# Seven merge-gate tiles of each layer move from the attention's filling into the rotary stage

## The chip, the cores and the metric

The kernel runs on one core of a Trainium2 chip. A core has five engines with an instruction queue each: TensorE (PE: matrix products; PEld is its weight load), VectorE (DVE), ScalarE (ACT), GpSimd (POOL) and SyncE (SP), which here only issues transfers. The metric is the device time of one execution in microseconds, lower is better.

## The reference

Two layers of a mixer act on 1024 tokens of a prompt and on 32 tokens of a running stream (1056 columns in all), with 1024 channels in float32. The part that matters here:

```
h = rmsnorm(x) * (1 + scale) + shift
u_a, z_a, b_a, a_a, q_b, k_b, v_b, z_b, g_a, g_b = split(h @ w_in)
o_a = gated_delta_rule(conv_silu(u_a), ...)      # branch A: a triangular inverse per chunk, a scan over chunks
q_b, k_b = rope(q_b), rope(k_b)                  # branch B: differential attention, 8 heads of two maps
o_b = softmax1(q_b k_b) v - lam * softmax2(...) v
merged = sigmoid(g_a) * (o_a @ w_proj_a) + sigmoid(g_b) * (o_b @ w_proj_b)
x = x + gate * (merged @ w_out)
```

Each of g_a and g_b has 1024 columns, that is eight tiles of 128. The change is about seven of the eight tiles of g_a.

## The kernel before, in words

Activations lie channel by channel, in three groups of tokens (384, 384 and 288 columns), each split into a high and a low part; a product in full precision is three products (high x high, high x low, low x high). One tile of a projection (128 output columns, 1024 channels, one token group) is thus 8 x 3 = 24 products into one PSUM bank. Weights come as float32 (`wraw`) and are split into `whi` (ScalarE) and `wlo` (GpSimd or VectorE).

A layer runs through these stages:

- A: for each of eight heads the projections of u_a, the convolution, and `k.T @ [k q]` in three passes (`ptk`, L599 on), which VectorE and ScalarE write to `rec` (two buffers, stored at L622) and `U` (stored as `ublk`, L629). Rotary pair 0 is already emitted here.
- B, the rotary stage: `rope_pair` (L786) for pairs 1 to 7, four of queries and keys each by turns (odd pairs are keys). For a token group it has two tiles `pr` of 24 products (L813 on); VectorE multiplies each by cosine and sine (`rt`, four a group); GpSimd makes two `ro` of the four; they are stored, and for keys TensorE transposes them (`ptk`, L830). Beside it `invert` (L646) inverts 128 unit lower triangles of 64 x 64, one to a partition: 63 steps, each an `itmp` (product) and an `X` (subtraction), the first 26 columns on VectorE, the others on GpSimd, and a copy `ub<-X` (L668) at its end. Two sections of eight steps are emitted after each pair; the instruction order on every engine is settled by a scheduler when the program is built.
- C1: merging the inverses, and the scan over chunks. Its first product is that of the values, `ptok`, which stands behind everything in B.
- C2: the attention, whose products wait for softmax on ScalarE and VectorE. TensorE's order is written out by hand in C1 and C2: `pad` takes independent products from a list of fillers (values, the gate tiles z_b, g_a, g_b, z_a by `zproj`, L1154, in the bank `pd`, and branch A's projection) and puts them between the attention's steps. What is left (`s.left`) is spread in equal shares over what is still to come, and `s.pad(1e9)` runs the remainder at the end.
- E, F: attention's projection, the merge, the output projection, and the next layer's norm.

PSUM has eight banks. Two of them belong to the pool `pd` (projections of all kinds, `pr` and `ptok` among them) for the whole program; the other pools are opened and closed by stage. A stage's pool that takes the banks of an earlier one waits for the last reader there. Small results (`ro`, `rt`, `zo`) share the eight buffers of the pool `ev`.

Of the kernel before, what the change touches and what calls it, by code (L numbers as in the profile page):

```python
# [10 lines left out]
F32 = mybir.dt.float32  # L11
F32R = mybir.dt.float32r
# [6 lines left out]
L = 2  # L19
# [19 lines left out]
class Net:  # L39
# [39 lines left out]
    def setup(s, st):  # L79
# [3 lines left out]
        s.pd = P("pd", 2, space=PSUM)  # L83
# [34 lines left out]
    def conditions(s, tmp):  # L118
        """The two conditioning vectors, channel by channel."""
# [86 lines left out]
    def pad(s, ns):  # L206
        """Independent products, as far as there are any, for this long on the tensor engine."""
# [20 lines left out]
    def mod_init(s, pool):  # L228
        """The two conditioning vectors, both parts of each, as stationary columns."""
# [9 lines left out]
    def mod_chunk(s, l, part, c):  # L239
        """256 columns of shift (part 0), scale (1) or gate (2), by channel."""  # L240
# [19 lines left out]
    def mod_gate(s, l):  # L260
        """The gate's rows, halved for the gates' 1 + tanh."""
# [9 lines left out]
    def mod_first(s, part, c, pool, wpool):  # L271
        """256 columns of the first layer's shift or scale, in plain float32."""
# [24 lines left out]
    def start(s, h, pool, wpool, xpool):  # L297
        """The first layer's activations, channel by channel as its scale and shift arrive."""
# [50 lines left out]
    def rstd(s, pool, ss, n, scale, add):  # L349
        """(ss * scale + add) ** -0.5; add: a number or an AP."""  # L350
# [17 lines left out]
    def norm_tile(s, pool, l, x, t, h, r):  # L368
# [12 lines left out]
        h = h if isinstance(h, list) else h(g)  # L381
# [8 lines left out]
    def gates(s, l, pool, h):  # L390
# [28 lines left out]
        # beta = 1 / (1 + exp(-b))  # L419
# [6 lines left out]
        # g = -exp(a_log) * softplus(a + dt_bias)  # L426
# [83 lines left out]
    def conv_head(s, l, pool, h, hd, cv, gates=None):  # L510
        """q, k and v of one head; with `gates`, the last token group comes after the others."""
# [33 lines left out]
    def gdn1(s, l, pool, h, hd, cv, gates=None):  # L545
# [5 lines left out]
        # token-major k, v and the squares of q and k  # L551
# [19 lines left out]
        # 1/|k| and its uses  # L571
# [13 lines left out]
        # q with its decay, channel-major  # L585
# [60 lines left out]
    def invert(s, l, pool):  # L646
        nc = s.nc
        for B, nb, src, xd, pdst in ((64, 128, s.ublk[l], s.xblk[l], s.pblk[l]), (32, H, s.ublks[l], None, s.pblks[l])):
# [25 lines left out]
    def merge_inverse(s, l, pool, hd):  # L674
        """The off-diagonal quarter of each chunk's inverse, and all of it to the scan's records."""
# [24 lines left out]
    def scan(s, l, pool, gap):  # L700
        """One (chunk, head) after the other; each one's three stages start a turn apart."""
# [9 lines left out]
        def first(c, hd):  # L711
# [11 lines left out]
            if c == 0:  # L723
                # the prompt's state is zero before it
# [61 lines left out]
    def rope_pair(s, l, pool, wpools, h, c_base, pr, dst, tabs, out):  # L786
        """Four (head, map) groups: tile A has their first halves, tile B the second ones."""
        nc = s.nc
        W = []
        for kk in range(2):  # L790
# [6 lines left out]
            if not out:  # L797
                # the queries' factor, a power of two
# [10 lines left out]
        for g, (t0, n) in enumerate(GROUPS):  # L809
# [3 lines left out]
            for e in range(2):  # L813
# [3 lines left out]
                for x, tab in enumerate((cos, sin)):  # L817
                    tmp = s.ev.tile([128, 384], F32, tag="ev", name=f"rt{e}{x}")
                    s.tt(tmp[:, :n], ps[:, :n], tab[:, sl], OP.mult)
                    tm.append(tmp)  # L820
            s.tt(o[0][:, :n], tm[0][:, :n], tm[3][:, :n], OP.subtract, eng=nc.gpsimd)
# [719 lines left out]
```

## Time and profile before

| | |
|---|---|
| runs | 3727.11, 3731.49, 3732.44 us (median 3731.49) |
| span of the profiled execution | 3730.3 us |
| busy share of the span | TensorE 93%, VectorE 62%, ScalarE 41%, GpSimd 37% |
| mean granted TensorE clock | 0.973 of full speed |
| stage B of layer 0, first `ptk` of the last head to first `ptok` | 526.7 to 750.3 us |
| the same of layer 1 | 2338.8 to 2561.2 us |
| attention C2, layers 0 and 1 | 1096 to 1731 us, 2870 to 3539 us |

The profiled execution is one of its own; its span is the time that the sums are made against, and the median of the runs is what a change is measured by. TensorE's share is a mean over stages: it is nearly full in C1, C2, E and F, and less so in A and B.

### The profile page before, as it was taken

The numbers are of one execution on the slowest core, as the hardware profiler recorded it, in microseconds if no ns is written. First come the engines' busy times: TensorE is split into PE (matmuls) and PEld (weight loads), VectorE is DVE, ScalarE is ACT, GpSimd is POOL, SyncE is SP. The second block draws the span as 40 slices with busy tenths as digits, with TensorE's granted clock in tenths as the row PEclk, the third lists the DMA queues.
The fourth block names the chain that finished last, engine by engine and source line by source line (L and its number), as shares of the span: only waits on it lengthen the run. The fifth ranks groups of instructions, "written<-read, shape, count | busy, mean of one in ns | idle before, by whom it ended". The sixth has DMA issues, their size and how long they took to land.

```text
span 3730.3 us, 58279 instructions
## 1 busy us (share of the span) xinstructions
PE 3465.2 (93%) x20752; PEld 3122.7 (84%) x20752; DVE 2301.0 (62%) x3874; ACT 1525.3 (41%) x4246; POOL 1370.8 (37%) x1259
## 2 busy tenths in 40 slices
PE   8888897899999999899999998879999999989999
PEld 6888897878978888789988888878898888878897
DVE  5677758832436667865456676787043666777554
ACT  4566541123534444433244656211354444444421
POOL 2456548701143343423002223792111443343310
PEclk9999999999999999999999999989999999999999
DMA  5445544266743334445443434424775333444554
GB/s 176 118 143 149 144 122 120 78 185 202 229 114 89 118 114 128 143 136 177 139 144 92 120 114 118 134 79 135 204 225 158 101 110 107 131 139 142 171 155 149
DMA packets 611307, 518.01 MB, mean 139 GB/s; under 512 B 103444, under 2 KB 563864, under 8 KB 610632
## 3 DMA queue, kind: packets, MB, share of 16 engines
q1 hardware_dynamic: 611016, 514.29, 46.7%
q8 instruction: 164, 2.69, 0.3%
q14 instruction: 127, 1.04, 0.1%
HBM read 333.84 MB, written 180.31 MB: 138 GB/s over the span
## 4 chain that ended last, share of the span: by engine, by line
PE 50%; DMA 9%; DVE 9%; POOL 4%; issue 4%; ACT 2%; SPq 1%; DVEq 0%; POOLq 0%; ACTq 0%
PE pd L72 25%; PE ptok L72 9%; PE psc L72 5%; PE pts L72 2%; PE pav L72 2%; DMA Gb<-grow 2%; DMA srec<-grec 2%; PE po L72 1%; PE pr L72 1%; PE pta L76 1%; DMA kraw<-kscr 1%; DVE qh L942 1%; DMA er<-rrow 1%; PE ptm L72 1%; POOL X L54 1%
## 5 line engine op out<-in xcount | busy, mean ns | idle before, releaser
L72 PE MATMUL pd<-h,whi 128*128 128x384 f32 (+1 forms) x5376 | 1405.8, 337 | 35.1 <-ACT u L69 28.5
L72 PEld LDWEIGHTS pd<-h,whi 128*128 128x128 f32 x5376 | 947.4, 193 | 61.5 <-ACT u L69 30.7
L72 PE MATMUL pd<-h,wlo 128*128 128x384 f32 (+1 forms) x2688 | 902.6, 336 | 0.0
L54 POOL TENSOR_TENSOR wlo<-wraw,whi 128x512 fp32r<-128x512 f32 (+1 forms) x220 | 432.6, 1975 | 503.9 <-ACT whi L69 461.1
L72 PEld LDWEIGHTS pd<-h,wlo 128*128 128x128 f32 x2688 | 516.9, 192 | 11.8 <-issue 8.1
L72 PE MATMUL pr<-h,whi 128*128 128x384 f32 (+1 forms) x1536 | 389.1, 338 | 30.5 <-DVE rt L54 30.4
L69 ACT CAST whi<-wraw 128x1024 fp32r<-128x1024 f32 (+1 forms) x304 | 259.3, 866 | 227.8 <-PE pd L72 77.8
L66 ACT ACTIVATE e<-psc,nm 32x160 f32<-32x160 f32 (+8 forms) x288 | 200.7, 700 | 290.0 <-DVE nm L1016 168.3
L72 PEld LDWEIGHTS pr<-h,whi 128*128 128x128 f32 x1536 | 279.0, 197 | 39.2 <-DVE rt L54 37.9
L72 PE MATMUL pr<-h,wlo 128*128 128x384 f32 (+1 forms) x768 | 257.8, 336 | 0.7 <-POOL wlo L54 0.7
L63 DVE SCALAR_TENSOR_TENSOR acc<-u,convT,acc 128x1059 f32<-128x1059 f32 x144 | 220.7, 1536 | 2.7
L72 PE MATMUL pd<-oa,whi 128*128 128x384 f32 (+1 forms) x768 | 196.2, 334 | 3.9 <-DVE egt L63 3.9
L72 PE MATMUL pd<-ob,whi 128*128 128x384 f32 (+1 forms) x768 | 181.9, 322 | 4.6 <-DVE egt L63 4.6
L54 DVE TENSOR_TENSOR wlo<-wraw,whi 128x1024 fp32r<-128x1024 f32 x84 | 107.6, 1281 | 121.3 <-ACT whi L69 121.2
L72 PE MATMUL ptok<-whi,h 128*128 128x512 f32 x512 | 164.8, 401 | 5.7 <-DVE rt L54 5.7
L54 DVE TENSOR_TENSOR itmp<-ub,X 128x624 f32<-128x624 f32 (+56 forms) x188 | 152.5, 811 | 15.3 <-DMA ub<-ublks 6.5
L72 PE MATMUL ptok<-whi,mg 128*128 128x512 f32 x512 | 158.7, 392 | 1.0 <-DVE y L54 1.0
L54 DVE TENSOR_TENSOR X<-X,itmp 128x624 f32<-128x624 f32 (+56 forms) x188 | 153.6, 817 | 5.0
L54 POOL TENSOR_TENSOR ro<-rt,rt 128x384 f32<-128x384 f32 (+1 forms) x96 | 115.5, 1222 | 102.5 <-issue 53.9
L72 PE MATMUL psc<-k,qh 128*128 128x512 f32 (+3 forms) x416 | 150.6, 394 | 2.3 <-ACT e L66 2.1
L72 PE MATMUL psc<-k,ql 64*128 64x512 f32 (+3 forms) x416 | 152.4, 448 | 0.0
L72 PEld LDWEIGHTS pr<-h,wlo 128*128 128x128 f32 x768 | 151.3, 197 | 1.1 <-POOL wlo L54 1.1
(308 smaller groups left out, 7121.8 us busy)
## 6 DMA issues: line engine op xcount, KB each, us to landing
wraw<-in_w_in SPq DMA_DIRECT2D x160, 512.0 KB
srec<-grec SPq DMA_DIRECT2D x128, 384.0 KB
grec<-rec SPq DMA_DIRECT2D x128, 192.0 KB
z<-zo SPq DMA_DIRECT2D x96, 192.0 KB
wraw<-in_w_ada SPq DMA_DIRECT2D x64, 256.0 KB
egt<-z SPq DMA_DIRECT2D x64, 192.0 KB
eo<-ob SPq DMA_DIRECT2D x60, 192.0 KB
Gb<-grow SPq DMA_DIRECT2D x16, 576.0 KB
```

The source lines that it names most:

```text
L54: (eng or s.nc.vector).tensor_tensor(out, a, b, op=op)
L63: s.nc.vector.scalar_tensor_tensor(out, a, sc, b, op0=op0, op1=op1)
L66: s.nc.scalar.activation(out, a, func, **kw)
L69: s.nc.scalar.copy(out, a)
L72: s.nc.tensor.matmul(out, lhsT, rhs, start=start, stop=stop)
L76: s.nc.tensor.transpose(out, a, s.ident[0:n, 0:n])
L942: s.nc.vector.tensor_copy(q[64 * u:64 * u + 64], raw[a])
```

## The change

`zproj` keeps eight tiles of g_b, z_a and z_b in the filling, but of g_a only the last. A new function `gate_tile` does the first seven, one for each rotary pair 1 to 7; its token groups run one by one in `rope_pair`, through the new argument `between`, after the group's `rt` and ahead of its `ro`. The gate's products go to the pool that the `pr` use, its tanh `zo` takes a seventh buffer of `ev` in each group, and its weights take the buffers of the pool that the pair doesn't use.

```diff
@@ rope_pair
+            if between:
+                between(g)
             s.tt(o[0][:, :n], tm[0][:, :n], tm[3][:, :n], OP.subtract, eng=nc.gpsimd)
@@ after zproj
+    def gate_tile(s, l, h, which, ti, pool):
+        (w,) = [s.wload(s.io["w_in"][l], 0, KT, (C_GA, C_GB)[which - 2] + ti * 128, 128, pool=pool, eng=s.nc.gpsimd, own_raw=False)]
+        def group(g):
+            t0, n = GROUPS[g]
+            ps = s.now(s.group(w, h, g))
+            o = s.ev.tile([128, 384], F32, tag="ev", name="zo")
+            s.act(o[:, :n], ps[:, :n], AF.Tanh, scale=0.5)
+            s.st.dma_start(out=s.zscr[l][which][ti][:, t0:t0 + n], in_=o[:, :n])
+        return group
@@ run, stage B
-                            drain(rope(n, [s.wp if n % 2 else v2] * 2, b2))
+                            own, other = (s.wp, v2) if n % 2 else (v2, s.wp)
+                            drain(rope(n, [own] * 2, b2, s.gate_tile(l, h, 2, n - 1, other)))
@@ run, fillers
-                    z = [(w, ti) for w in (1, 2, 3, 0) for ti in range(8)]
+                    z = [(w, ti) for w in (1, 2, 3, 0) for ti in range(8) if w != 2 or ti == 7]
-                s.left = 24 * T / 2.4 * 40 + 2 * (8 * 24 + 16) * 512 / 2.4
+                s.left = 24 * T / 2.4 * 33 + 2 * (8 * 24 + 16) * 512 / 2.4
```

The pool `pd` becomes one of each stage: two banks in A, four in B, two in C, two in E and F; B's transposes get a third bank.

```diff
@@ setup
-        s.pd = P("pd", 2, space=PSUM)
@@ run, stage A and stage B
-                    s.pt = psum(st, f"pta{l}", 3)
+                    s.pd, s.pt = psum(st, f"pda{l}", 2), psum(st, f"pta{l}", 3)
-                    s.pt = psum(st, f"ptb{l}", 2)
+                    s.pd, s.pt = psum(st, f"pdb{l}", 4), psum(st, f"ptb{l}", 3)
```

And the next layer's activations no longer rotate through an extra place; they are written over the merged ones, in the place of the same token group.

```diff
-            place = [(pr_, "g0", 384), (pr_, "g1", 384), (pg2, "g2", SZ[2])]
+            place = [(pr_, f"g{g}", w) for g, w in enumerate(SZ)]
@@ run, stage F
-                    place = [(p0, "x", 384), place[0], place[1]]
-                        s.tail(l, f2, f1, xs, None if l == L - 1 else pool(st, f"xo{l}", 2), merged, grow)
+                        s.tail(l, f2, f1, xs, None if l == L - 1 else pool(st, f"xo{l}", 2), merged, merged)
```

The other edits of the diff take comments out. How the order of instructions moves:

TensorE before, at the end of stage A in layer 0: `pr` are products of rotary pair 1, `ptk` those of the last head's `k.T @ [k q]`.

```order
L72 MATMUL pr<-h_126,wlo 128x384
L72 MATMUL pr<-h_127,whi 128x288
L72 MATMUL pr<-h_130,whi 128x288
L72 MATMUL ptk<-kqh 128x256
L72 MATMUL ptk<-kql,kqh 128x256
L72 MATMUL ptk<-kqh,kql 128x256
L72 MATMUL ptk<-kql,kqh 128x256
L72 MATMUL ptk<-kqh,kql 128x256
L72 MATMUL ptk<-kqh 32x2x32
L72 MATMUL pr<-h_127,wlo 128x288
L72 MATMUL pr<-h_127,whi 128x288
```

They stand mixed. TensorE of the change, the end of the same `ptk`:

```order
L72 MATMUL ptk<-kqh 32x2x32
L72 MATMUL ptk<-kql,kqh 128x256
L72 MATMUL ptk<-kqh,kql 128x256
L72 MATMUL ptk<-kql,kqh 128x256
L72 MATMUL ptk<-kqh,kql 128x256
L72 MATMUL ptk<-kql,kqh 32x2x32
L72 MATMUL ptk<-kqh,kql 32x2x32
L72 MATMUL pr<-h_119,whi 128x384
L72 MATMUL pr<-h_122,whi 128x384
L72 MATMUL pr<-h_119,wlo 128x384
```

Here no `pr` stands among the `ptk`; the first of pair 1 comes behind the last of them.

TensorE of the change, layer 0, a little later: the last products of pair 1's second tile of the first token group, then the gate tile's first ones (`pd`), 24 of them in a row.

```order
L72 MATMUL pr<-h_119,whi 128x384
L72 MATMUL pr<-h_122,whi 128x384
L72 MATMUL pr<-h_119,wlo 128x384
L72 MATMUL pd<-h_119,whi 128x384
L72 MATMUL pd<-h_122,whi 128x384
L72 MATMUL pd<-h_119,wlo 128x384
L72 MATMUL pd<-h_119,whi 128x384
```

In the order before, the pair's second token group stood at this place.

VectorE before, the end of the first inverse in layer 0 (with numbers of the buffers): `pr_7853` is the second tile of the second token group of pair 7.

```order
L54 TENSOR_TENSOR itmp0_6029<-ub_6023,X_6024 128x78
L54 TENSOR_TENSOR X_6024<-X_6024,itmp0_6029 128x3x26
L54 TENSOR_TENSOR itmp0_6029<-ub_6023,X_6024 128x52
L54 TENSOR_TENSOR rt10_7878<-pr_7853,cos_5779 128x384
L54 TENSOR_TENSOR rt11_7880<-pr_7853,sin_5781 128x384
L54 TENSOR_TENSOR X_6024<-X_6024,itmp0_6029 128x2x26
L54 TENSOR_TENSOR itmp0_6029<-ub_6023,X_6024 128x26
L54 TENSOR_TENSOR X_6024<-X_6024,itmp0_6029 128x26
L668 COPY ub_6023<-X_6024 128x64x64
L54 TENSOR_TENSOR rt00_7931<-pr_7906,cos_5779 128x288
```

VectorE of the change, the end of the same inverse: `pr_7363` is the first tile of the second token group of pair 4, and `pr_7392` the second one.

```order
L54 TENSOR_TENSOR rt00_7388<-pr_7363,cos_5780 128x384
L54 TENSOR_TENSOR itmp0_6034<-ub_6028,X_6029 128x130
L54 TENSOR_TENSOR rt01_7390<-pr_7363,sin_5782 128x384
...
L54 TENSOR_TENSOR itmp0_6034<-ub_6028,X_6029 128x52
L54 TENSOR_TENSOR X_6029<-X_6029,itmp0_6034 128x2x26
L54 TENSOR_TENSOR itmp0_6034<-ub_6028,X_6029 128x26
L54 TENSOR_TENSOR X_6029<-X_6029,itmp0_6034 128x26
L666 COPY ub_6028<-X_6029 128x64x64
L54 TENSOR_TENSOR rt10_7417<-pr_7392,cos_5780 128x384
```

The copy at the inverse's end stood behind the `rt` of the 40th of the 42 rotary tiles of pairs 1 to 7; now it stands behind those of the 21st. Between the first step of the inverse and that copy VectorE had 70 `rt` in layer 0 and 68 in layer 1; it has 42 in both now, and the same 126 operations of the inverse.

## Rows read from the trace of the kernel before

**Rows 1.** Windows: stretch, length, busy us (count) of PE, PEld, DVE, ACT, POOL; clock, DMA, GB/s.
```profile
526.70:750.30 223.60, 185.10 (x1096) 177.60 (x1095) 186.41 (x242) 40.77 (x92) 173.41 (x148) 0.95 0.37 106
1096.00:1731.00 635.00, 603.92 (x3479) 520.97 (x3478) 433.62 (x784) 274.99 (x729) 247.49 (x218) 0.98 0.42 127
2338.80:2561.20 222.40, 187.57 (x1105) 179.17 (x1103) 186.56 (x244) 43.66 (x96) 174.35 (x148) 0.94 0.38 108
```

**Rows 2.** Waits of TensorE, rotary stage of layer 0: us, times, longest.
```profile
PE ptk L76 <- POOL ro L54: 21.6, 6, 6.8
PE pr L72 <- DVE rt L54: 9.4, 9, 1.9
```

**Rows 3.** Waits of VectorE while the first inverse runs.
```profile
DVE rt L54 <- PE pr L72: 10.0, 4, 5.3
DVE rt L54 <- POOL ro L54: 6.6, 4, 2.9
```

**Rows 4.** The inverse of layer 0: its window, and VectorE's groups by line.
```profile
562.40:746.00 183.60, 148.10 (x861) 141.62 (x859) 163.21 (x197) 27.02 (x55) 154.28 (x128) 0.93 0.33 96
...
L54 DVE TENSOR_TENSOR rt<-pr,cos 128x384 f32<-128x384 f32 (+1 forms) x34 | 17.7, 519 | 16.6 <-PE pr L72 10.0 <-POOL ro L54 6.6
L54 DVE TENSOR_TENSOR wlo<-wraw,whi 128x1024 fp32r<-128x1024 f32 x2 | 3.0, 1512 | 0.0
```

**Rows 5.** Timeline of TensorE, products of the rotary stage: start, length, operation.
```profile
495.26 0.51 PE L72 MATMUL pr<-h,whi 128*128 128x384 f32 x2
495.79 0.51 PE L72 MATMUL pr<-h,whi 128*128 128x384 f32 x2
...
518.78 0.43 PE L72 MATMUL pr<-h,whi 128*128 128x288 f32 x2
519.18 0.43 PE L72 MATMUL pr<-h,whi 128*128 128x288 f32 x2
```

**Rows 6.** Timelines of TensorE, SyncE's queue and VectorE around the tail of stage A.
```profile
526.73 0.28 PE L72 MATMUL ptk<-kqh 128*128 128x256 f32 x1
...
550.37 1.29 SPq L629 DMA_DIRECT2D ublk<-U  x2
...
562.49 0.23 DVE L54 TENSOR_TENSOR itmp<-ub,X 128x63 f32<-128x63 f32 x1 [3.80 <-DMA ub<-ublk]
```

**Rows 7.** Timelines of VectorE and TensorE at the end of the first inverse.
```profile
742.47 0.21 DVE L54 TENSOR_TENSOR itmp<-ub,X 128x52 f32<-128x52 f32 x1
742.60 0.55 DVE L54 TENSOR_TENSOR rt<-pr,cos 128x384 f32<-128x384 f32 x1
743.06 0.55 DVE L54 TENSOR_TENSOR rt<-pr,sin 128x384 f32<-128x384 f32 x1
743.76 1.03 DVE L54 TENSOR_TENSOR itmp<-ub,X 128x26 f32<-128x26 f32 x1
745.81 3.79 DVE L668 COPY ub<-X 128x4096 f32<-128x4096 f32 x1
...
750.30 0.73 PE L72 MATMUL ptok<-whi,h 128*128 128x512 f32 x2 [2.25 <-DVE rt L54]
```

**Rows 8.** GpSimd beside it: timeline, and groups by line of the stretch of rows 4.
```profile
743.74 1.99 POOL L54 TENSOR_TENSOR ro<-rt,rt 128x384 f32<-128x384 f32 x2 [6.04 <-issue]
...
L54 POOL TENSOR_TENSOR ro<-rt,rt 128x384 f32<-128x384 f32 (+1 forms) x34 | 44.9, 1340 | 19.9 <-issue 19.9
L54 POOL TENSOR_TENSOR wlo<-wraw,whi 128x512 fp32r<-128x512 f32 x20 | 36.8, 1852 | 3.4 <-ACT whi L69 3.4
```

**Rows 9.** The cast of a gate tile's weights in the attention: count, ns min/median/max.
```profile
L54 POOL TENSOR_TENSOR wlo<-wraw,whi x21: 2364/2391/2577, 1099.6 to 1526.1; 128x1024 fp32r<-128x1024 f32 x21
```

**Rows 10.** Attention of layer 0: TensorE's waits ahead of `pta`, and the softmax's last steps.
```profile
PE pta L76 <- DVE aT L54: 15.3, 8, 6.7
PE pta L76 <- DVE e L63: 3.5, 2, 2.0
...
L63 DVE SCALAR_TENSOR_TENSOR e<-e,cf x72: 351/754/2901, 1105.8 to 1693.3; 32x160 f32<-32x160 f32 x8, 128x128 f32<-128x128 f32 x8, 128x256 f32<-128x256 f32 x8, 128x384 f32<-128x384 f32 x8
```

More of the change, by code (lines that the diff above doesn't have):

```diff
@@ L380, in norm_tile @@
                   scale=s.mA[l][:, j, k:k + 1], bias=s.md[l][:, k, j:j + 1])
-        h = h if isinstance(h, list) else h(g)
         hi, lo = h[0][g][:, :, o:o + n], h[1][g][:, :, o:o + n]
@@ L783, in scan, with rope_pair @@
                 last(c, 0 if (i - 5) % H == 0 else 4)
-    def rope_pair(s, l, pool, wpools, h, c_base, pr, dst, tabs, out):
+    def rope_pair(s, l, pool, wpools, h, c_base, pr, dst, tabs, out, between=None):
         nc = s.nc
@@ L1302, in run @@
             SZ = [n for _, n in GROUPS]
-            keep, extra = ExitStack(), ExitStack()
+            keep = ExitStack()
             pr_ = pool(keep, "acts", side="right")
-            pg2 = pool(extra, "act2", side="right")
-            place = [(pr_, "g0", 384), (pr_, "g1", 384), (pg2, "g2", SZ[2])]
+            place = [(pr_, f"g{g}", w) for g, w in enumerate(SZ)]
             def acts(nm):
@@ L1314, in run @@
             with ExitStack() as st:
-                s.pb = psum(st, "pb0", 2)
-                s.pt = psum(st, "pt0", 1)
+                s.pd, s.pb, s.pt = psum(st, "pd0", 2), psum(st, "pb0", 2), psum(st, "pt0", 1)
                 tmp = pool(st, "start", 1)
@@ L1327, in run, with rope @@
                 tabs = []
-                def rope(n, wpools, out):
+                def rope(n, wpools, out, between=None):
                     pr, qk = divmod(n, 2)
-                    return s.rope_pair(l, out, wpools, h, (C_QB, C_KB)[qk], pr, (s.qscr, s.kscr)[qk][l], tabs, qk == 1)
+                    return s.rope_pair(l, out, wpools, h, (C_QB, C_KB)[qk], pr, (s.qscr, s.kscr)[qk][l], tabs, qk == 1, between)
                 with ExitStack() as st:
-                    s.pt = psum(st, f"pta{l}", 3)
+                    s.pd, s.pt = psum(st, f"pda{l}", 2), psum(st, f"pta{l}", 3)
                     g1 = pool(st, f"a1{l}", 1)
@@ L1407, in run @@
                 s.fill = fillers()
-                s.left = 24 * T / 2.4 * 40 + 2 * (8 * 24 + 16) * 512 / 2.4
+                s.left = 24 * T / 2.4 * 33 + 2 * (8 * 24 + 16) * 512 / 2.4
                 order = ExitStack()
                 order.enter_context(tc.manual_schedule(engines={mybir.EngineType.PE}))
+                pdc = ExitStack()
+                s.pd = psum(pdc, f"pdc{l}", 2)
                 with ExitStack() as st:
@@ L1442, in run @@
                 order.close()
-                nx = ExitStack()
-                p0 = pool(nx, f"x{l}")
+                pdc.close()
                 with ExitStack() as te:
+                    s.pd = psum(te, f"pde{l}", 2)
                     xs = pool(te, f"xs{l}", 2)
@@ L1449, in run @@
                         p12 = pool(tb, f"ob{l}")
-                        ob = [[p0.tile([128, KT, 384], F32R, tag=f"x{a}", name=f"ob{a}0")]
-                              + [p12.tile([128, KT, SZ[g]], F32R, name=f"ob{a}{g}") for g in (1, 2)] for a in range(2)]
+                        ob = [[p12.tile([128, KT, SZ[g]], F32R, name=f"ob{a}{g}") for g in range(3)] for a in range(2)]
                         eb = pool(tb, f"eb{l}", 6)
@@ L1459, in run @@
                             drain(s.proj(l, ob, 1, [ti], merged, s.mscr[l], False))
-                    hn = [[], []]
-                    place = [(p0, "x", 384), place[0], place[1]]
-                    def grow(g):
-                        while len(hn[0]) <= g:
-                            p, tag, w = place[len(hn[0])]
-                            for a in range(2):
-                                hn[a].append(p.tile([128, KT, w], F32R, tag=f"{tag}{a}", name=f"h{a}{len(hn[a])}"))
-                        return hn
                     with ExitStack() as st:
@@ L1474, in run @@
                         f2 = s.Multi(pool(st, f"f2{l}", 2), f1, ("x", "y", "ss", "rs1", "xn"))
-                        s.tail(l, f2, f1, xs, None if l == L - 1 else pool(st, f"xo{l}", 2), merged, grow)
-                if l == L - 1:
-                    nx.close()
-                extra.close()
-                h, extra = hn, nx
+                        s.tail(l, f2, f1, xs, None if l == L - 1 else pool(st, f"xo{l}", 2), merged, merged)
+                h = merged
             keep.close()
```

## The prediction

> **What bounds the kernel now.** I read the windows by stage first, then the waits of the stage that has room, then its lines. In the attention (1096 to 1731 us) TensorE is busy for 603.92 of 635 us; the stage is full, and a product that is taken out of its filling shortens it. The rotary stage is the loose one: 185.10 of 223.60 us in the first layer, 187.57 of 222.40 in the second [rows 1]. The waits say for what TensorE idles there: transposes of keys wait for GpSimd's `ro` (21.6 us), products wait for a bank that VectorE's `rt` has still to read (9.4 us) [rows 2]; behind both stands VectorE, since `ro` waits for `rt`. VectorE's own waits in that stage come to 10.0 us for products and 6.6 us for `ro` [rows 3], against 163.21 us of work in the 183.60 us between the inverse's first product and its end [rows 4]. So the stage's clock is VectorE's chain: 126 operations of the inverse (63 steps of two, L654 on), which follow one on the other, with the `rt` set between them in a fixed order.
>
> **The change, part by part.** *What leaves the filling.* Three products of 384 columns start 0.53 us after the three before, three of 288 columns 0.40 us [rows 5], so 24 of them take 4.21 and 3.2 us, and a gate tile (two groups of 384 and one of 288) 11.6 us. Seven are 81.4 us a layer, and they leave a stage that is full: −81.4. Nothing else covers them there, so I take this as a whole.
>
> *What the rotary stage costs TensorE now.* A rotary pair has two tiles a group: 23.25 us; seven pairs and seven gate tiles are 244. The four key pairs among them have 72 transposes of 128 columns; by the pace above that is 0.06 us each, and I take twice that, since a short product may be held by its weights: 8 us. Sum 252.
>
> *The tail of stage A.* The order shows that the last head's `ptk` now stand alone and the first `pr` of pair 1 behind them all, because the banks of the rotary stage are those of the stage before. Today the tail runs from the first `ptk` at 526.73 to the store of the last `U` at 550.37, TensorE filled all the way by pair 1; the first product of the inverse follows at 562.49, 12.1 us behind the store [rows 6]. Alone, the tail goes at the pace of its two record buffers and of the small instructions that fill and store them. Bounds: 17 us (an estimate: 23.6 less some 7 that VectorE gives there to pair 1's `rt` and to waits for its products) and the 23.6 us of today; I take 19.5, nearer to the lower, since only small instructions are left in the queues. The first product of the inverse then comes at 31.5 us after the first `ptk`. TensorE stands idle in the tail for some 15.5 us (19.5 less the `ptk` themselves) that pair 1 filled before.
>
> *VectorE's chain.* An `rt` of 384 columns is followed by the next 0.46 us later [rows 7], one of 288 columns by its length some 0.36, 0.43 in the mean; 68 are 29 us, the two weight casts 3.0 [rows 4]. So of 163.2 us the inverse itself has 131. The order now sets 42 `rt` among the inverse's products instead of 68: 18 us. Idle: 20.4 us today, of which the 10.0 for products should go, because four banks instead of two let TensorE run further ahead; I take 10, with 5 and 20 as ends. Less GpSimd work lies beside the chain: 21 `ro` instead of 34, at 1.34 us that is 17 us less; and some six fewer weight casts of the pairs at 1.85 us against three of the gates' at 2.4, another 4 [rows 8, 9]. What this is worth shows at the end of the chain: with GpSimd still, an `itmp` of 52 columns takes 0.21 us; beside GpSimd's two `ro` from 743.74 to 745.73 one of 26 columns takes 1.03 [rows 7, 8]. By that, 2 us of GpSimd cost the chain about 1.5, and 21 would give back 16; most of the products are far longer than these and run beside GpSimd's own share of the inverse, which stays, so I take −5, with 0 and −16 as ends. The chain: 131 − 5 + 18 + 10 = 154 us, and its 42nd `rt` stands some 4 us ahead of its end (the 3.79 us copy [rows 7] is the end): 150.
>
> The Trainium skill ("SBUF — State Buffer", section SBUF: two separate sides) says that a VectorE operation with two SBUF inputs and a GpSimd operation that reads SBUF lock each other out for a whole instruction. The 1.03 us above agree with it; by the rule in full the term would be the −16 named as an end, and the sum 22 us lower.
>
> *What is left behind the chain.* The 42nd `rt` reads the 21st of the 42 rotary tiles. With four banks TensorE can be three tiles further, and no more. Left are the second tile and the gate of that pair's last group (2 × 3.2), three pairs with gates (3 × 34.85) and 36 transposes (4): 115 us, in which TensorE is the bound (per group it then has 12.6 us of products against 1.9 us of `rt`). With 4 us for the end of the copy, the first value product `ptok` comes at 31.5 + 150 + 115 + 4 = 300.5 us after the first `ptk`, against 223.6 and 222.4 today: +77.5. The step that makes this so is the wait for the 21st tile's `rt`: TensorE could be done up to it at 19.5 + 137 = 156.5 us, VectorE lets it through at 181.5, so 25 us are lost.
>
> *The attention with less filling.* The filling between its steps is spread over a smaller total, about a quarter less. Today transposes wait 15.3 us in 8 places for `aT` and only twice, 3.5 us, for the last step of a softmax, of which there are 72 [rows 10]: nearly all have cover to spare. I take +5 a layer, with 2 and 20 as ends (20 if each of the ten waits grew by 2 us). In C1 nothing changes.
>
> *The rest.* The gates' tanh and their stores go to ScalarE and SP, which are far from busy in the rotary stage (ScalarE 40.77 of 223.60 us [rows 1]): 0; the 21 tanh would have to take over 8 us each to make ScalarE the bound there. The in-place activations let the next layer's last tokens no longer run beside twenty gate products, and the start loses the like: +3 once, ends 0 and 6.
>
> Sum: 77.5 − 81.4 + 5 = +1.1 a layer, +2.2 for both, +3: +5.2 on the profiled span of 3730.3, so 3735.5. That execution lies 1.2 us under the median of the runs (3731.5): **3737 us**. It is so near to nothing because what the products save in the attention, they cost once more in a stage whose idle time they were to fill: TensorE's idle time there stays between 45 and 50 us, it only moves to the tail and to the wait in the middle.
>
> **The rivals.** *R1, faster: the four banks and the gates fill the waits.* TensorE becomes the bound in the whole rotary stage, if VectorE's chain is at its 42nd `rt` by 156.5 us. Then `ptok` comes at 19.5 + 252 + 3 = 274.5, +51.5, and the layer gains 24.9: 3731.5 − 49.8 + 3 = 3685. For it: both of today's waits [rows 2] are for buffers. Against it: 163 busy of 183.6 us on VectorE [rows 4], and the order. The sign turns when the chain is some 3 us shorter a layer than I have it, and to be measured as faster it takes 6. A GpSimd relief near its −16 does this alone.
>
> The Trainium skill ("Perfetto Trace Analysis", Identifying Performance Opportunities, Optimization Strategy) says that a gap which repeats on the engine that should be saturated can mean too little SBUF or PSUM for the next tile; by that rule R1's 3685 is what the change gives. The repeating waits of [rows 2] agree with it, the busy share of VectorE in [rows 4] does not.
>
> *R2, slower: the idle time of VectorE stays.* A group now takes seven of the eight `ev` buffers instead of six, so an `rt` waits for the `ro` before it and its store. If idle stays at 20.4, the layer loses 10 more: 3737 + 20 = 3757. For it: today's 6.6 us for `ro` [rows 3]. Against it: a gate product of 4.2 us lies between the groups and gives that time back. It decides from 11 us of idle upwards. *R3, slower: the attention's cover is too thin*, +20 instead of +5: 3767, or 3787 with R2.
>
> **How the numbers follow.** The forecast's own case (3724 to 3752) gets 0.43, R1 and all between it and 3724 get 0.33, R2 and R3 0.24. A measurement of this kernel tells about 0.2% from no change, 7.5 us. Of the forecast's case 0.26 lie within that and 0.17 above: faster 0.33, same 0.26, slower 0.41. The range leaves 0.1 at each end: on the low side two thirds of the way from 3724 into R1, 3698; on the high side R3, 3768.
>
> **What would show it.** Right: the tail's `ptk` alone, in some 19 to 20 us, with TensorE idle between; the first `itmp` 31 to 32 us after the first `ptk`; `pr` waiting for `rt` for over 20 us in sum while the inverse runs; `ptok` 300 us after the first `ptk`; the attention shorter by about 76 us. Wrong: `ptok` by 285 us (R1: no long wait of `pr` for `rt`); VectorE's idle in the inverse near 20 (R2); waits of `pta` and `pav` in the attention above 45 us (R3). What would most easily make it wrong is the length of the inverse's products beside another mix on GpSimd, which no row of before shows.

## The result: 2.7% slower, and the profile after

The changed kernel takes 3833.2 us (median of 4 runs, 3829.2 to 3836.3) against 3732.0: ratio 1.0269, 95% interval 1.0255 to 1.0284, that is 101 us. The forecast was 3737, in a range of 3698 to 3768. The profiled span is 3834.5 us, 104.2 over the one before. The heads of the two pages, before and after:

```profile
span 3730.3 us, 58279 instructions
...
PE 3465.2 (93%) x20752; PEld 3122.7 (84%) x20752; DVE 2301.0 (62%) x3874; ACT 1525.3 (41%) x4246; POOL 1370.8 (37%) x1259
```

```profile
span 3834.5 us, 58245 instructions
...
PE 3511.5 (92%) x20752; PEld 3165.1 (83%) x20752; DVE 2312.4 (60%) x3874; ACT 1521.1 (40%) x4246; POOL 1377.3 (36%) x1259
```

TensorE is 46.3 us busier than before with as many instructions (x20752), so its products took longer and did not become more. Windows of the rotary stage (from the first `ptk` of the last head to the first `ptok`), of the inverse in it, and of the attention, layers 0 and 1; columns as in [rows 1]; below them the attention before, both layers, from its first `pta` on, as in the two lines after:

```profile
529.00:850.00 321.00, 273.83 (x1610) 265.76 (x1609) 226.56 (x312) 60.02 (x125) 195.50 (x158) 0.92 0.38 109
557.30:728.10 170.80, 139.97 (x815) 136.52 (x815) 155.59 (x169) 26.60 (x51) 142.04 (x112) 0.91 0.33 92
1198.00:1776.30 578.30, 534.16 (x2934) 450.08 (x2935) 418.72 (x774) 252.91 (x690) 219.39 (x204) 0.94 0.40 120
3052.40:3632.40 580.00, 532.17 (x2935) 445.86 (x2936) 419.25 (x773) 253.00 (x691) 219.55 (x204) 0.95 0.40 120
```

```profile
1106.30:1731.00 624.70, 595.62 (x3431) 513.42 (x3432) 430.17 (x778) 272.82 (x723) 240.15 (x214) 0.98 0.42 126
2913.20:3533.20 620.00, 592.77 (x3430) 511.26 (x3431) 430.01 (x776) 272.93 (x723) 239.55 (x214) 0.98 0.42 127
```

The rotary stage takes 321 us, 97 more than in [rows 1]. The attention is 46 and 40 us shorter than its 624.70 and 620.00 us before, at a granted clock of 0.94 and 0.95 of full speed instead of 0.98. TensorE's waits in the rotary stage of layer 0 and in its attention (us, times, longest):

```profile
PE pr L72 <- POOL wlo L54: 17.4, 2, 12.5
PE ptk L76 <- POOL ro L54: 16.5, 11, 4.3
...
PE pr L72 <- DVE rt L54: 3.4, 1, 3.4
...
PE pta L76 <- DVE e L63: 14.7, 4, 4.8
PE pta L76 <- DVE aT L54: 13.5, 7, 6.0
PE pta L76 <- ACT oTb L69: 6.5, 6, 2.2
PE pav L72 <- DVE aT L54: 6.1, 3, 2.9
PE pd L72 <- DVE egt L63: 4.8, 1, 4.8
```

In the rotary stage a single wait of 12.5 us for the low part of a pair's own weights (`wlo`) is new; in the same stage before such waits came to 0.7 us. For `rt`, which the prediction had TensorE wait for, it is 3.4 us. In the attention the wait for the softmax's last step, 3.5 us in 2 places in [rows 10], is 14.7 in 4, and waits for `oTb` are new. The timelines of TensorE, where the tail of stage A ends and the first value product begins, and of VectorE at the start and the end of the first inverse and of the second one (8 partitions):

```profile
545.83 0.99 PE L72 MATMUL pr<-h,whi 128*128 128x384 f32 x2
...
849.96 0.63 PE L72 MATMUL ptok<-whi,h 128*128 128x512 f32 x2
...
557.32 0.21 DVE L54 TENSOR_TENSOR itmp<-ub,X 128x63 f32<-128x63 f32 x1
...
721.31 0.55 DVE L54 TENSOR_TENSOR rt<-pr,sin 128x384 f32<-128x384 f32 x1
724.19 3.91 DVE L666 COPY ub<-X 128x4096 f32<-128x4096 f32 x1
...
743.88 1.08 DVE L54 TENSOR_TENSOR itmp<-ub,X 8x31 f32<-8x31 f32 x1 [9.39 <-DMA ub<-ublks]
...
780.16 1.12 DVE L666 COPY ub<-X 8x1024 f32<-8x1024 f32 x1
```

The first `ptk` of that head starts at 529.04 us. So the tail takes 16.8 us, the inverse begins 28.3 us after it, the last `rt` ahead of the copy stands at 721.31, and `ptok` comes at 849.96, 320.9 us after the start.

From first and last starts on TensorE's timeline, the whole difference of 104 us adds up so (layer 0 / layer 1, after less before): up to the last head's first `ptk` +2.3 / +4.4; from there to the first `ptok` +97.3 / +93.9; from there to the last product of branch A's projection, which ends the attention's filling, −54.4 / −44.4; the last stage +5.0.

TensorE's time in the two stages splits into three parts: idle time, time lost to the lower clock (in steps of 4 us, busy time multiplied by the share of the clock that is missing), and the rest, products at full clock. In the rotary stage these are 47.2, 16.0 and 257.8 us in layer 0 (before 38.5, 9.1 and 176.0), and 44.2, 13.9 and 258.2 in layer 1 (before 34.8, 8.9 and 178.7). The products grow by 82 and 80 us, the price of the seven gates; waits and clock add 16 and 14.

### The profile page after: what moved, and what is told of

Its sections match the earlier page's. It is cut to its first block, busy times and chain, and to the rows that moved or that the text cites. A ratio compares the mean times of both kernels' runs of the same rounds, so it can differ in the third digit from the quotient of the medians.

```text
span 3834.5 us, 58245 instructions
## 1 busy us (share of the span) xinstructions
PE 3511.5 (92%) x20752; PEld 3165.1 (83%) x20752; DVE 2312.4 (60%) x3874; ACT 1521.1 (40%) x4246; POOL 1377.3 (36%) x1259
## 5 line engine op out<-in xcount | busy, mean ns | idle before, releaser
L72 PE MATMUL pd<-h,whi 128*128 128x384 f32 (+1 forms) x2688 | 715.7, 343 | 22.1 <-ACT u L69 19.3
L72 PE MATMUL pd<-mg,whi 128*128 128x384 f32 (+1 forms) x2688 | 704.9, 340 | 13.3 <-ACT u L69 13.3
L72 PEld LDWEIGHTS pd<-h,whi 128*128 128x128 f32 x2688 | 484.1, 197 | 35.6 <-ACT u L69 20.8
L72 PEld LDWEIGHTS pd<-mg,whi 128*128 128x128 f32 x2688 | 479.1, 195 | 25.7 <-ACT u L69 14.2
L72 PE MATMUL pd<-h,wlo 128*128 128x384 f32 (+1 forms) x1344 | 457.7, 341 | 0.5 <-POOL wlo L54 0.5
L72 PE MATMUL pd<-mg,wlo 128*128 128x384 f32 (+1 forms) x1344 | 455.4, 339 | 0.0
L72 PEld LDWEIGHTS pd<-h,wlo 128*128 128x128 f32 x1344 | 264.3, 197 | 6.7 <-issue 3.7
L72 PEld LDWEIGHTS pd<-mg,wlo 128*128 128x128 f32 x1344 | 261.9, 195 | 6.3 <-issue 4.0
L72 PE MATMUL pr<-h,whi 128*128 128x384 f32 (+1 forms) x768 | 193.4, 337 | 8.8 <-DVE rt L54 8.8
L72 PE MATMUL pr<-mg,whi 128*128 128x384 f32 (+1 forms) x768 | 194.9, 338 | 7.0 <-DVE rt L54 7.0
```

Source lines behind the costliest of these rows:

```text
L72: s.nc.tensor.matmul(out, lhsT, rhs, start=start, stop=stop)
```

## The experiments

Each time is compared with the kernel before, run beside it. Most experiments have one run; where the kernel before was run seven times beside them, its times lie 12 and 17 us apart, so a difference under some 10 us says nothing by itself. "B" is the time from the last head's first `ptk` to the first `ptok` in layer 0, "C" that from there to the last `pd<-oa`, layers 0 / 1, both worked out from starts in the traces. Before: B 223.6, C 980.7 / 972.0. Changed: B 320.9, C 926.3 / 927.6.

**What the parts of the change cost alone.** First the changed kernel with all gates back in the filling, so that only pools and places stay:

```diff
-                            drain(rope(n, [own] * 2, b2, s.gate_tile(l, h, 2, n - 1, other)))
+                            drain(rope(n, [own] * 2, b2))
-                    z = [(w, ti) for w in (1, 2, 3, 0) for ti in range(8) if w != 2 or ti == 7]
+                    z = [(w, ti) for w in (1, 2, 3, 0) for ti in range(8)]
-                s.left = 24 * T / 2.4 * 33 + 2 * (8 * 24 + 16) * 512 / 2.4
+                s.left = 24 * T / 2.4 * 40 + 2 * (8 * 24 + 16) * 512 / 2.4
```

> The changed kernel with the seven gate tiles back in the attention's filling: what is left of the change are the PSUM pools by stage (four banks in the rotary stage) and the places of the activations. Theory G (the moved gates cost the 101 us): within 15 us of the kernel before, 3720 to 3747, the rotary stage 215 to 232 us from the last head's first ptk to the first ptok, TensorE's tail alone for 17 us. Rival P (the pools by stage cost it, since TensorE stands idle in the tail of stage A): 3765 or more.

Measured (e1) 3786.7 against 3741.3: ratio 1.0118 (1.0091 to 1.0144), +45 us. Theory G is refuted as it stood: without one gate moved, a good part of the loss is there. B is 243.4, C 980.3 / 973.5 as before. The inverse ends at 738.6, 11 us earlier than before, but then 31 us pass to `ptok`, 22.5 of them rotary products and transposes, where there were none in [rows 7]: 122 rotary products now stand behind the inverse, about as many as pair 1 put into the tail (114). Of the 20 us that B grows by, 12.7 are idle time of TensorE (8.6 of it in the tail, where there was none) and 7.8 the lower clock.

The other half, the kernel before with the gates moved (the edits of `rope_pair`, `gate_tile`, the filling and `s.left` in the first diff) and nothing else:

> The kernel before with the seven gate tiles moved, and nothing else of the change: two banks for the whole program, pair 1 mixed into the tail of stage A. Theory G: 3810 to 3850, the attention as in the changed kernel (some 47 us shorter than before, not 81), the rotary stage over 310 us. Rival P: 3775 or less, since the tail is filled again.

Measured (e2) 3856.9 against 3741.3, +116: more than the whole change, a little above theory G's range and far from rival P. B is 329.9, C 930.9 / 926.4. The tail is not filled again as it was: 42 products of pair 1 stand in it in layer 0 and 50 in layer 1, where the kernel before has 114 and 132. So the parts do not add up: +45 and +116 alone, +101 together; once the gates are there, the rest of the change takes back 9 and 14 us of B.

The pools alone, with the old places of the activations (the two edits of the rotary stage; others give the other stages their pools):

```diff
-        s.pd = P("pd", 2, space=PSUM)
-                    s.pt = psum(st, f"ptb{l}", 2)
+                    s.pd, s.pt = psum(st, f"pdb{l}", 4), psum(st, f"ptb{l}", 3)
```

> The kernel before with the PSUM pools by stage alone: four banks for the rotary stage, three for its transposes, the old places of the activations, no gate moved. Theory T (the banks of the rotary stage are those of stage A, so pair 1's 23 us of products leave the tail and come behind the inverse): the rotary stage some 20 us longer a layer, 30 to 45 us over the kernel before of the same call, the last stage as before. Rival (the new places of the activations cost most of the 45 us of pools and places together): 12 us over it or less.

Measured (e9) 3761.9 against 3733.6, +28, a little under the range. B is 243.9, 20 more than before, as expected. The last stage is 197.7 us as before, against 202 to 205 in every run that has the new places (the changed kernel, e1, e3, e5, e6, e8) and 196 to 200 in every run without: the places cost 5 us there. Between e9 and e1 lie another 10 us from the end of layer 0's attention to layer 1's last head (604.5 and 614.9 us; 607.7 before), from one run of each.

**What leaves the attention.** The kernel before without the seven gates anywhere:

```diff
-                    z = [(w, ti) for w in (1, 2, 3, 0) for ti in range(8)]
+                    z = [(w, ti) for w in (1, 2, 3, 0) for ti in range(8) if w != 2 or ti == 7]
                 elif which:
-                    s.st.dma_start(out=s.zscr[l][which][ti][:, t0:t0 + n], in_=o[:, :n])
+                    for tj in range(8) if which == 2 else [ti]:
+                        s.st.dma_start(out=s.zscr[l][which][tj][:, t0:t0 + n], in_=o[:, :n])
```

> The kernel before without the seven gate tiles of each layer: they are left out of the filling and computed nowhere (the eighth tile's result is stored in the places of all eight). It prices what leaves the attention, with the rotary stage untouched. Theory C (thinner filling lets TensorE wait more, and its clock is granted at half speed behind the waits): the layer gains 45 to 55 us instead of 81, 3620 to 3642. The prediction's own term (full stage, 5 us of waits): 3732 - 2 x 76 = 3580.

Measured (e4) 3648.1 against 3741.3: −93, or 47 a layer for 81 us of products, as theory C had it (45 to 55; its 3620 to 3642 was reckoned from a kernel before of 3732) and far from my 3580. C is 931.8 / 931.1. Its attention, by window:

```profile
1108.10:1684.60 576.50, 526.75 (x2936) 441.39 (x2936) 418.14 (x777) 255.84 (x695) 223.89 (x207) 0.96 0.42 123
2869.60:3446.20 576.60, 528.09 (x2935) 442.24 (x2935) 419.58 (x774) 255.05 (x693) 222.50 (x207) 0.95 0.41 122
```

TensorE idles 49.8 and 48.5 us (577 less busy time), against 29.1 and 27.2 before, at a clock of 0.96 and 0.95. The lower clock takes 21 and 23 us, 12 and 9 before. So this loss stands without any change in the rotary stage: some 21 us of new waits, and 9 and 14 more of products at the lower clock. In such stretches 0.5 of full speed is granted, 1.2 GHz instead of 2.4, and products of 384 columns start 0.32 us apart instead of 0.17.

**How many gates, and where.** The changed kernel with three moved tiles only (the fillers' list keeps the others):

```diff
-s.gate_tile(l, h, 2, n - 1, other)
+s.gate_tile(l, h, 2, n - 1, other) if 1 <= n <= 3 else None
-                s.left = 24 * T / 2.4 * 33 + 2 * (8 * 24 + 16) * 512 / 2.4
+                s.left = 24 * T / 2.4 * 37 + 2 * (8 * 24 + 16) * 512 / 2.4
```

> The changed kernel with three moved gates instead of seven, beside pairs 1 to 3; the other four tiles stay in the filling. In the order 46 rt stand ahead of the inverse's copy (42 with seven gates, 68 with none). Theory S (each rotary tile whose rt stands behind the inverse costs its TensorE time once more, wherever the gates are): rotary stage some 275 us from the last head's first ptk, 60 to 80 us over the kernel before of the same call. Rival I (TensorE idles in the first pairs anyway, so gates there are free): 45 us over it or less, below the 45 of the pools alone less what the attention gains.

> The same three moved gates' worth, beside pairs 5 to 7. In the order 60 and 62 rt stand ahead of the inverse's copy. Theory S: within 20 us of the run with pairs 1 to 3, since what the later rt save behind the inverse the gates take there. Rival I: 30 us or more above that run, since here the gates stand where TensorE is the bound.

Measured (e5, e6) 3756.1 and 3759.9 against 3743.0: +13 and +17. B is 275.0 and 275.1, theory S's figure to a microsecond, and it makes no difference beside which pairs the gates stand, which refutes rival I's reason. But the time is some 50 us lower than S had it and inside rival I's 45, since the attention gives far more for three tiles than I thought: C is 931.5 / 935.0, 49 and 38 under e1. Its windows of the attention:

```profile
1148.80:1731.90 583.10, 558.29 (x3217) 476.48 (x3218) 413.54 (x774) 261.03 (x707) 230.28 (x208) 0.98 0.43 127
2963.30:3551.10 587.80, 563.23 (x3217) 480.53 (x3218) 415.60 (x774) 261.36 (x707) 230.04 (x208) 0.97 0.43 126
```

TensorE is idle for 24.8 and 24.6 us, no more than before, and the clock is 0.98 and 0.97. So 35 us of products taken out are worth 38 to 49 here, and the 46 us of the four others only 5 to 7 more (C of the changed kernel). That it is over 35 is partly e1's clock: the lower clock costs 18.6 and 12.3 us in its attention, 8.9 and 13.7 in that of e5. B, on the other hand, pays for every tile: e1 to e5 31.6 us for three, e1 to the changed kernel 77.5 for seven, 10.5 and 11.1 a tile of 11.6 us.

**What holds the rotary stage.** Three runs ask for GpSimd. In the first the low part of the gates' weights is a ScalarE copy of them:

```diff
-        (w,) = [s.wload(..., pool=pool, eng=s.nc.gpsimd, own_raw=False)]
+        s.cp(hi, raw)
+        s.cp(lo, raw)
```

> The changed kernel, but the low part of the moved gates' weights is a ScalarE copy of the weights instead of GpSimd's subtraction (so the seven gates are wrong in value, with the same products on TensorE). Theory W (GpSimd is full beside the inverse, and the gates' casts push the pairs' casts and ro back, as the 12.5 us wait of pr for wlo says): the rotary stage shorter by 12 to 30 us a layer, 3775 to 3810. Rival V (VectorE's chain and the order of rt in it alone set the stage): within 8 us of the changed kernel, 3825 to 3841.

Measured (e3) 3819.7 against 3741.3, +78; the changed kernel is 101 over its own, so this is 23 us less, and outside of both ranges. B is 312.4 / 309.6, 8.5 and 6.7 us shorter than in the changed kernel, less than theory W's 12: the gates' casts hold the stage up, but by little. The wait of `pr` for `wlo` is still there (11.2 us): it is not the gates' casts that make it. What stands ahead of that `wlo` is on GpSimd's timeline in the changed kernel:

```profile
655.86 1.35 POOL L54 TENSOR_TENSOR X<-X,itmp 128x280 f32<-128x280 f32 x1
657.17 3.04 POOL L54 TENSOR_TENSOR ro<-rt,rt 128x288 f32<-128x288 f32 x2
660.18 1.98 POOL L54 TENSOR_TENSOR wlo<-wraw,whi 128x512 fp32r<-128x512 f32 x1
```

The cast of the pair's `wlo` that ends TensorE's wait (from 649.7 to 662.2) stands behind two `ro` and nine steps of the inverse, which fill GpSimd's queue from 643.21 on.

Then the whole 64 x 64 inverse on VectorE, in the kernel before and in the changed one (for 63 steps GpSimd's columns go to VectorE):

```diff
-    CUT = 26
+    CUT = 64
```

> The kernel before with the whole 64 x 64 inverse on VectorE (the share of GpSimd, columns 26 on, is gone). Theory L (VectorE's operations with two SBUF inputs and GpSimd's lock each other out, so that two engines on the inverse win little): the inverse's chain within 15 us of its 187, the kernel within 30 us of the kernel before. Rival Q (the two engines work side by side): the chain takes over GpSimd's 9100 columns twice, some 19 us at a column a nanosecond, plus what it did, 200 to 215 us a layer, and the kernel is 25 to 60 us slower.

> The changed kernel with the whole 64 x 64 inverse on VectorE. If GpSimd's queue is what holds the pairs' casts and ro back there (the 12.5 us wait of pr for wlo, ptk for ro 14.9): the rotary stage shorter by 10 to 30 us a layer, 20 to 60 us below the changed kernel. If VectorE's chain alone sets it: longer by some 15 us a layer.

Measured (e7, e8) 3718.1 and 3801.9 against 3743.0: −25, where theory L had no more than ±30 and rival Q a loss, and +59, 42 us better than the change. In e8 B is 299.1 / 294.1, 22 us shorter than in the changed kernel in both layers, and the wait of `pr` for `wlo` is 5.8 us instead of 17.4; 48 `rt` stand ahead of the inverse's copy in its trace, 40 in the changed kernel's, so that a free queue and the shifted order are not told apart. The window of the inverse in the kernel before with this edit, and TensorE's waits in that stage and in the merge behind it (us, times, longest):

```profile
564.00:748.40 184.40, 165.96 (x984) 154.69 (x983) 177.90 (x204) 34.43 (x67) 98.90 (x58) 1.00 0.43 121
```

```profile
PE pr L72 <- DVE rt L54: 8.4, 8, 1.6
PE ptk L76 <- POOL ro L54: 5.0, 5, 2.0
...
PE ptm L72 <- DMA mu<-u: 17.2, 1, 17.2
```

VectorE does GpSimd's part of the inverse too and takes 184.4 us for it with four more `rt` among it, where the two took 187.1 together ([rows 6, 7]). So GpSimd's help was worth nothing. What the edit brings is GpSimd's queue: TensorE waits 5.0 us for `ro` instead of 21.6 [rows 2], and `ptok` comes 29 us earlier; 17.2 us of that are lost again, since the merge now waits for the inverse. C is 995.7 / 1001.0, 15 and 29 us longer, so that by the traces layer 1 gains nothing; against the trace of the kernel before e7 is 14 us shorter, against the run beside it 25. Why the help is worth nothing stands on GpSimd's timeline in the changed kernel, around a stretch in which VectorE stood still:

```profile
634.43 1.69 POOL L54 TENSOR_TENSOR X<-X,itmp 128x357 f32<-128x357 f32 x1
636.20 1.55 POOL L54 TENSOR_TENSOR itmp<-ub,X 128x352 f32<-128x352 f32 x1
637.83 0.88 POOL L54 TENSOR_TENSOR X<-X,itmp 128x352 f32<-128x352 f32 x1
638.79 0.79 POOL L54 TENSOR_TENSOR itmp<-ub,X 128x345 f32<-128x345 f32 x1
643.21 1.69 POOL L54 TENSOR_TENSOR X<-X,itmp 128x336 f32<-128x336 f32 x1
644.98 1.48 POOL L54 TENSOR_TENSOR itmp<-ub,X 128x325 f32<-128x325 f32 x1
...
635.40 1.71 DVE L54 TENSOR_TENSOR itmp<-ub,X 128x936 f32<-128x936 f32 x1
637.03 0.44 DVE L54 TENSOR_TENSOR rt<-pr,cos 128x288 f32<-128x288 f32 x1
642.34 0.46 DVE L54 TENSOR_TENSOR rt<-pr,sin 128x288 f32<-128x288 f32 x1 [4.86 <-POOL ro L54]
```

From 637.5 to 642.3 VectorE waits for `ro`. GpSimd's `X` and `itmp` of 350 columns take 1.69 and 1.55 us while VectorE works, 0.88 and 0.79 while it waits, and 1.69 and 1.48 again after. So GpSimd takes about twice as long beside VectorE. VectorE loses less: its 936 columns take 1.71 us above, where in e7, while GpSimd does nothing from 636.70 to 642.09, 999 columns take 1.18:

```profile
632.97 3.73 POOL L54 TENSOR_TENSOR ro<-rt,rt 128x384 f32<-128x384 f32 x2 [2.09 <-issue]
642.09 3.79 POOL L54 TENSOR_TENSOR ro<-rt,rt 128x384 f32<-128x384 f32 x2 [5.38 <-issue]
...
638.61 1.18 DVE L54 TENSOR_TENSOR itmp<-ub,X 128x999 f32<-128x999 f32 x1
```

The Trainium skill ("SBUF — State Buffer", section SBUF: two separate sides) calls the port pair that a VectorE operation with two SBUF inputs shares with a GpSimd operation that reads SBUF an exclusive lock. These rows agree with it in that each holds the other up.

Last, the changed kernel without the steps of the inverses:

> The changed kernel with the steps of both inverses left out (only their copies stay), so nothing but TensorE's products, rt, ro and casts is left in the rotary stage. If TensorE's own work is the floor there, as the prediction's rival R1 has it: first ptk to ptok 270 to 280 us instead of 321, and the kernel 80 to 105 us under the changed kernel, that is level with the kernel before or slightly over it: seven gates in the rotary stage could not have paid even with the inverse free. If the rt behind the inverse are all that costs: under 240 us, and the kernel under 3700.

Measured (e13) 3752.9 against 3738.1, +15, as the first theory had it. B is 274.4 us, and TensorE's work is nearly all of it:

```profile
528.30:802.70 274.40, 261.19 (x1609) 257.36 (x1608) 65.41 (x124) 60.37 (x125) 98.26 (x84) 0.96 0.42 128
```

In layer 1 it is 269.5. So 274.4 and 269.5 us are TensorE's floor with seven gates and these pools, 51 and 47 over the stage before. The two inverses add the other 46 us. Even the floor takes as much as the attention gives for seven tiles (54 and 44 us).

**A version that beats both.** Three tiles, two banks of their own for them so that pair 1 may stay in the tail, and the inverse on VectorE or not. These are the edits of the banks, made to the kernel before along with `gate_tile` for three tiles:

```diff
+            pd, s.pd = s.pd, s.pg
             ps = s.now(s.group(w, h, g))
+            s.pd = pd
-                    s.pt = psum(st, f"ptb{l}", 2)
+                    s.pt, s.pg = psum(st, f"ptb{l}", 2), psum(st, f"pg{l}", 2)
```

> The kernel before with three gate tiles beside pairs 1 to 3, whose products have two banks of their own in the rotary stage; the rotary products stay in the two shared banks, so pair 1 stays in the tail. If tail and gates simply add: the run with pairs 1 to 3 and all of the change (13 us over the kernel before) less the 40 us of pools and places: 20 to 35 us under the kernel before. If the four banks were what made three gates cheap: not under it.

> The same with the whole inverse on VectorE, 62 rt ahead of its copy instead of 48. If the attention gains 40 us a layer for the first three tiles and the rotary stage, with GpSimd's queue free, pays their 35 us or less: 35 to 70 us under the kernel before. If GpSimd was not the limit: as the run without this edit.

> The same with the gates beside pairs 5 to 7, 66 and 64 rt ahead of the inverse's copy. Here the first value product came 25 us ahead of the inverse's end in the run with the inverse on VectorE alone, and the merge of the inverses waits for that; gates there fill the wait: 40 to 75 us under the kernel before, 5 to 15 under the run with pairs 1 to 3.

Measured (e10 to e12) 3741.8, 3703.5 and 3682.7 against 3733.6: +8, −30 and −51. The first was expected 20 to 35 under, and at +8 it may as well be level: B is 266.3, so three gates cost 43 us with two banks for the rotary tiles and 32 with four. The second falls a little short of its range, the third is in its own, 21 us under the second instead of 5 to 15. Its B is 239.0, and its inverse ends at 747.3, ahead of `ptok` at 766.2, so that the merge no longer waits for it.

> The whole inverse on VectorE, own banks for the gates, four gates beside pairs 4 to 7. If the attention's gain is used up with three tiles and the rotary stage pays some 11 us a tile: 10 to 25 us over the run with pairs 5 to 7. If the fourth tile still gains: under it.

> The run with the whole inverse on VectorE and three gates beside pairs 5 to 7 once more, timed in rounds: 1.1 to 1.5 per cent under the kernel before.

The third version timed again (e15) is 3688.4 against 3738.1, ratio 0.986 (0.9841 to 0.9879), as expected: 50 us faster than the kernel before. A fourth tile (e14) gives 3729.4 beside it, 41 us worse; it misses my 10 to 25 on the bad side. Most of that is the rotary stage: B is 252.1 / 255.2 against 238.4 / 235.3, 14 and 20 us for a tile of 11.6. C is 938.3 / 946.2 against 937.9 / 945.8, so the attention gives nothing for the fourth tile in these two runs. Attention by window with three tiles moved (e15, first two lines) and with four:

```profile
1110.10:1704.10 594.00, 564.39 (x3219) 482.01 (x3220) 414.35 (x780) 264.35 (x712) 234.08 (x211) 0.97 0.43 128
2897.30:3490.00 592.70, 561.73 (x3218) 479.17 (x3219) 415.57 (x775) 263.67 (x711) 233.09 (x211) 0.98 0.43 127
```

```profile
1129.50:1720.60 591.10, 557.53 (x3147) 473.46 (x3148) 432.28 (x777) 263.04 (x707) 224.85 (x209) 0.96 0.42 124
2930.20:3530.10 599.90, 563.56 (x3147) 478.02 (x3147) 432.22 (x776) 263.17 (x707) 226.97 (x210) 0.95 0.42 123
```

With 71 products less, TensorE is busy for 557.53 and 563.56 us instead of 564.39 and 561.73 and idle for 33.6 and 36.3 instead of 29.6 and 31.0, and the two stages together are 4 us longer, though 23 us of products are gone: the clock fell from 0.97 and 0.98 to 0.96 and 0.95. e12, the same kernel as e15, differs from it by 4 and 7 us in these windows, so a single run of four tiles doesn't place an edge to the tile. What all runs together show is where the gain ends: C is 971 to 981 us with no tile moved (before, e1, e9), 931 to 946 in the six runs with three, 938 and 946 with four, and 922 to 932 in the six with seven moved or left out (the changed kernel, e2, e3, e4, e8, e13).

## Why the prediction was wrong, point by point

The forecast was +5.2 us on the span, the trace shows +104.2. Of the 99 us between, the attention makes 54, the rotary stage 36, the rest 9.

- **What leaves the attention: −81.4 + 5 forecast, −54.4 and −44.4 measured.** This step failed, and its premise with it ("the stage is full, and a product that is taken out of its filling shortens it"). It holds for some three tiles (e5: 38 to 49 us for 35) and not for the others (e4: 47 us for 81 with nothing else changed). Waits grew by 15 and 21 us in the windows of the attention, where I took 5, with 2 and 20 as ends; what I had no term for is the granted clock. By steps of 4 us the lower clock takes 30 and 27 us there, 12 and 9 before. The clock column of [rows 1] never entered the sum.
- **The rotary stage as a whole: +77.5 forecast, +97.3 and +93.9 measured.** TensorE's idle time came out as forecast (47.2 and 44.2 us; I had 45 to 50), but in other places. Of the 20 us in layer 0, 16.0 are again the clock, without a term; the products are right, 258 us where I had 256 with those of the tail. The wait that I named as the step which makes it so, 25 us at the 21st tile for its `rt`, is not there: `pr` waits 3.4 us for `rt`. TensorE waited for GpSimd instead, 17.4 us for `wlo` and 16.5 for `ro`, and for neither did the sum have a term.
- **The tail: 31.5 us to the first step of the inverse forecast, 28.3 and 24.4 measured.** Right in kind, 3 and 7 us shorter than I had it, and so was the order's word that pair 1 leaves the tail. What that costs by itself, B +20, is shown by e9, without any gate.
- **VectorE's chain: 150 us to the 42nd `rt` forecast, 164.5 measured** (721.8 less 557.3). Mis-sized, by three things. The inverse's own steps up to the copy take 134.5 us (151.7 busy less 40 × 0.43; two of the 42 `rt` stand ahead of the first step), where I had 131 and took 5 off for less GpSimd work: per microsecond GpSimd is as busy as before (142.0 of 170.8 us; 154.28 of 183.60 in [rows 4]). Idle is 15 us instead of 10; R2's mechanism, `rt` behind `ro`, is in it with 6.2 us, as much as in [rows 3]. And I took the 3.79 us copy off at the end, though the window of [rows 4] ends where the copy starts, so that my 131 never held it.
- **Behind the chain: 119 us forecast, 128 measured.** TensorE is busy for 121.5 of the 128 us. It had not run three tiles ahead, so some 28 products more were left than I had; 4.9 us go to one more wait for `wlo`, 1.6 to other waits and 3 to the lower clock. My 4 us for the end of the copy are not there: TensorE does not wait for it.
- **R1 (3685)** needed a chain that ends in time, and did not come; its floor of 274.5 us was met (e13: 274.4 and 269.5), to the tenth by luck: TensorE idled 13.2 us in layer 0, where the sum had 15.5 in the tail alone, and lost 7 to the clock, for which it had nothing. But with it the kernel would not be at 3685: e13 is at +15, for the attention's gain that R1 counted on is not there. **R3** was the right place, with its price taken from waits alone: the waits of `pta` and `pav` came to 42 us, under the 45 that I had set as its sign.
- **The rest: +3 forecast, +11.7 measured** (2.3, 4.4 and 5.0); 5 of them are the new places of the activations in the last stage. The 2.3 are within what single runs differ by: up to the last head's first `ptk`, before any change, they take 525.1 to 530.3 us.

What stays open: waits and lower clock grow together in the attention, and no run changes one without the other, so that the clock's part is measured but not what makes it fall. Whether the thinner filling, spread in another way than in equal shares, would keep more of the gain was not tried either, and on the rotary stage e8 doesn't tell GpSimd's freed queue from the `rt` that moved ahead of the copy with it.

## What to carry to other kernels

Work that fills an engine's waits is not worth its own time to the last piece: here three tiles of seven brought theirs, and the rest came back as waiting and as a slower clock. How many pieces pay is found by taking out two or three, not all. A price for products should reckon with the granted clock of the stage that they leave and of the one that they enter; the rows by window show it. Before moving work into a stage, take its other work away on the chip once: the floor that is left (here 274 us) says at once whether the move can pay. And where two engines hold each other up as these two did, count them as one: give the work to one of them, and let the other's queue run free.

## What the runs showed that I had not expected

- Moving GpSimd's columns of the inverse to VectorE left the inverse as long as it was (184.4 against 187.1 us), and the kernel was 25 us faster in a single run.
- TensorE was as long busy with four tiles moved as with three (557.53 and 563.56 us against 564.39 and 561.73), with 71 products less; the granted clock was 0.96 and 0.95 against 0.97 and 0.98.
- The two halves of the change cost +45 and +116 us alone and +101 together.
